# First mixer and first products of a two-layer decoder: VectorE's and ScalarE's queues laid by hand, and small modulation sums moved to ScalarE

## The chip, the cores and the metric

The kernel runs on one core of one Trainium2 chip. A core has TensorE (PE, matmuls), VectorE (DVE), ScalarE (ACT), GpSimd (POOL) and SyncE (SP, which here issues the loads and stores). Each engine takes its own queue in order; engines wait for each other by semaphores. The metric is the time of one execution in device microseconds (us), as the median of several runs.

## The reference

A decoder of two layers on 512 tokens of width 1024, in float32. Each layer has a mixer and an MLP, both behind an RMS norm whose result is scaled and shifted by a modulation that is computed from a vector `c`. The first layer's mixer is pooling: for each of four groups of 256 features a running mean over a window of 2, 4, 8 or 16 tokens, less the token itself, then a 256x256 product. The second layer's mixer is a gated unit (`sgu`), which the change does not touch.

```python
c_act = jax.nn.silu(c)
for i in range(DEPTH):
    mod = c_act @ ada_w[i] + ada_b[i]
    sh1, sc1, g1, sh2, sc2, g2 = jnp.split(mod, 6, axis=-1)
    h = modulate(rmsnorm(x, norm_mix_g[i]), sh1, sc1)
    ...
    x = x + g1[:, None, :] * y
    h = modulate(rmsnorm(x, norm_mlp_g[i]), sh2, sc2)
    x = x + g2[:, None, :] * sq_relu_mlp(h, mlp_w1[i], mlp_w2[i])
return rmsnorm(x, final_g)
```

`modulate(h, sh, sc)` is `h * (1 + sc) + sh`; `sq_relu_mlp` is `square(relu(h @ w1)) @ w2`.

## The kernel before

**Stages.** The kernel works through the first mixer (lines 177 to 376), the first products of the first MLP (the "sweep", lines 379 to 401), the rest of the first MLP, the second mixer and the second MLP. A large product is made of three matmuls in a fast format (`mm3`, lines 125 to 127): each operand is split into a high part (`h`, a copy by ScalarE in the fast type) and a low part (`l`, the remainder, by VectorE). `split` (lines 116 and 117) does it for weights.

**The modulation.** A column of 128 values of `mod` is the sum, over the 1024 entries of `c_act` (spread over all partitions as `cb`), of the products with a transposed weight tile. `column` (line 249) and `ada_tile` (line 147) load a 512 KB tile and do this in one VectorE instruction with an accumulator. `finish_mods` (lines 132 and 136) adds the bias and makes `scl = (1 + sc) * gain`.

**The first mixer.** `row`, `x` and the bands (triangles of 1/window, built by GpSimd) come first; `squares` (lines 209, 211) and `power` (line 168, on GpSimd) give each token's norm `rt`, which is multiplied into the bands (`bandr`, line 235). Then, for each group g of 256 features:

- `gains(g)`: the gate g1 of the group, spread over partitions and multiplied into the pooling weights `pw` (lines 298, 301). For g = 0 and 1 TensorE makes it (lines 285, 286); for g = 2 and 3 VectorE makes two columns, ScalarE writes them on a diagonal `dgg` (line 295) and TensorE spreads them (line 296).
- `windows(g)`: the windowed means by TensorE, straight from `x` (line 271).
- `modulation(g)`: four columns, bias and scale (lines 249, 257, 259).
- `pooled(g)`: the shift's part `b0` (lines 314, 315) and then ScalarE's scaling out of PSUM into `pd` (line 318).
- `group(g)`: the product (line 328), its addition to `x` (line 329) and the squares for the next norm (lines 209, 211). All squares write a common scratch tile `sq`, so they follow each other.
- `feature_major(g)`: TensorE's transposes of `x` (line 337) and ScalarE's copy into `xf` (line 338).

At the end `s3` collects the sums of squares (lines 364 to 366), `power` makes `r4`, four diagonals (lines 373, 375) and four small matmuls (line 376) spread it as `rb`.

**The sweep.** Step k (0 to 7) takes 128 features: two columns of modulation (`ada_tile`), the load and split of the weights `w1s[k]` (`sweep_w`, lines 387 to 391), `norm_fm` (line 381 `ht`, line 382 `hh`, line 383 `hl`) and 21 matmuls of 512 columns into seven PSUM banks.

**What sets the order.** TensorE's queue is in the order of the program (`manual_schedule(engines={PE})`). The queues of VectorE, ScalarE and SyncE are made by a scheduler, which may put an instruction of a later step ahead of one that is not ready by its own estimate. Weight and modulation tiles live in rotating buffers: `w4` (three of 4 KB per partition) and `wh`, `wl` (five each). `get_any` hands out these 13 in turn, in the order in which the program asks. A load waits in SyncE's queue until its buffer is free, and holds up the loads behind it.

```python
slots = [(w4, "w4")] * 3 + [(wts, "wh"), (wts, "wl")] * 5
...
for k in range(KD):
    for j in range(2):
        ada_tile(0, 24 + 2 * k + j, ada0[16 + 2 * k + j], get_any)
    wk = sweep_w(k)
    norm_fm(k)
    for f in range(SWEEP):
        mm3(sweep[f], cut(wk, ALL, slice(P * f, P * f + P)), (hh[:, k], hl[:, k]), k == 0, k == KD - 1)
```

Of the kernel before, what the change touches and what calls it, by code (L numbers as in the profile page):

```python
# [14 lines left out]
P = 128  # L15
# [28 lines left out]
def c_g(n, k):  # L44
    return 24 * n + 16 + k
# [3 lines left out]
def decoder_kernel(ctx: ExitStack, tc: tile.TileContext, xtok, vecs, rows, fgrow, ada0, adag, ada1, pool_w, w1s, w1, w2, w2e, w_v, w_u, w_o, wsT, lnp, bs, out):  # L49
# [127 lines left out]
    with tc.tile_pool(name="st", bufs=1) as st, tc.tile_pool(name="st2", bufs=2) as st2:  # L177
# [45 lines left out]
        for n in range(2):  # L223
            pc = bank("pc")
            T.matmul(pc, ones[0:1, :], row[0:1, D + S + S * n : D + 2 * S + S * n], start=True, stop=True)
            A.activation(psb[:, S * n : S * n + S], pc, AF.Copy)
# [4 lines left out]
        rt = power(v0, NT)  # L231

# [18 lines left out]
        def modulation(g):  # L251

            c = slice(4 * g, 4 * g + 4)
            pm = sm.tile([P, 4], F32, name="pm4", tag="pm4")
            for j in range(4):
                column(ada0[4 * g + j], pm[:, j : j + 1])
            V.tensor_tensor(mods[0][:, c], pm, vec[:, V_ADAB + c.start : V_ADAB + c.stop], ALU.add)
            k = slice(2 * g, 2 * g + 2)
# [3 lines left out]
        b0 = st.tile([P, KD], F32, name="b0")  # L262
        xf = st.tile([P, KD, S], F32, name="xf")
        ssg = st.tile([P, NT, 4], F32, name="ssg")

        def window(k):

            po = bank("pq")
            for t in range(NT):
                n = P if t == NT - 1 else W  # L270
                T.matmul(po[:, P * t : P * t + n], x[:, t, P * k : P * k + P], bandr[:, t, k // 2, 0:n], start=(t == 0), stop=(t == NT - 1), skip_group_check=True)  # L271
            return po


        ON_PE = 2

        def gains(g):

            po = bank("pg", xz)[:, 0:256]
            if g < ON_PE:  # L280
                for j in range(2):
                    r = get_any().rearrange("p (k c) -> p k c", k=4)
                    nc.sync.dma_start(r, adag[g, j])
                    for k in range(4):
                        T.matmul(po, cab[:, 4 * j + k], r[:, k], start=(j + k == 0), stop=False)
                T.matmul(po, ones[0:1, :], row[0:1, D + 256 * g : D + 256 * g + 256], start=False, stop=True)
            else:
                pm = sm.tile([P, 2], F32, name="pmg", tag="pmg")
                dg = st2.tile([P, 2, P], F32, name="dgg", tag="dgg")
                for j in range(2):  # L290
                    k = 2 * g + j
                    column(ada0[32 + k - 2 * ON_PE], pm[:, j : j + 1])
                V.tensor_tensor(pm, pm, vec[:, V_ADAB + c_g(0, 2 * g) : V_ADAB + c_g(0, 2 * g) + 2], ALU.add)
                for j in range(2):
                    A.activation(dg[:, j], ident, AF.Copy, scale=pm[:, j : j + 1])
                T.matmul(po, ones, dg, start=True, stop=True)
            gp = st2.tile([P, 256], F32, name="gp", tag="gp")
            V.tensor_tensor(gp, po, psb[:, 256 * g : 256 * g + 256], ALU.mult)
            c = slice(2 * g, 2 * g + 2)
            nc.sync.dma_start(pw[:, c], pool_w[:, c])  # L300
            V.tensor_tensor(pw[:, c], pw[:, c], gp.unsqueeze(1).to_broadcast([P, 2, 256]), ALU.mult)

        pqs, pds = {}, {}

        def windows(g):
            for k in (2 * g, 2 * g + 1):
                pqs[k] = window(k)

        def pooled(g):

            win = 2 << g

            bg, sh = b0[:, 2 * g : 2 * g + 2], mods[0][:, 4 * g + 1 : 4 * g + 4 : 2]
            V.tensor_scalar(bg, sh, float(win), 1.0 / win, ALU.mult, ALU.mult)
            V.tensor_tensor(bg, bg, sh, ALU.subtract)
# [4 lines left out]
        def group(g):  # L320

            c = slice(256 * g, 256 * g + 256)
            for h in range(2):
                po = bank("po", xz).rearrange("p (t c) -> p t c", t=2)
# [4 lines left out]
                V.tensor_tensor(x[:, 2 * h : 2 * h + 2, c], x[:, 2 * h : 2 * h + 2, c], po, ALU.add)  # L329
                for t in (2 * h, 2 * h + 1):  # L330
                    squares(ssg[:, t, g : g + 1], t, c, V if (g, t) in ((3, 1), (3, 3)) else A)

        def feature_major(g):
            for k in (2 * g, 2 * g + 1):
                px = bank("px")
                for t in range(NT):
                    T.transpose(px[:, P * t : P * t + P], x[:, t, P * k : P * k + P], ident)
                A.activation(xf[:, k], px, AF.Copy)
# [27 lines left out]
        V.tensor_tensor(s3, s3, ssg[:, :, 3], ALU.add)  # L366
        feature_major(3)
        r4 = power(s3, NT)
        diag = st.tile([P, NT, P], F32, name="diag")
        rb = bank("rb", xz)  # L370
        for t in range(NT):
# [4 lines left out]
            T.matmul(rb[:, tok[t]], ones, diag[:, t], start=True, stop=True)  # L376


        def norm_fm(k):
            t = st2.tile([P, S], F32, name="ht", tag="ht")  # L380
            V.scalar_tensor_tensor(t, xf[:, k], scl[0][1][:, k : k + 1], rb, ALU.mult, ALU.mult)
            A.activation(hh[:, k], t, AF.Identity, bias=mod(0, c_sh(1, k)))  # L382
            V.scalar_tensor_tensor(hl[:, k], t, mod(0, c_sh(1, k)), f32(hh[:, k]), ALU.add, ALU.subtract)  # L383

        def sweep_w(k):
            r = w4.tile([P, D], F32, name="raw", tag="w4")
            nc.sync.dma_start(r[:, 0 : P * SWEEP], w1s[k])
            h, l = wpair()
            c = slice(0, P * SWEEP)
            A.activation(h[:, c], r[:, c], AF.Copy)  # L390
            V.tensor_tensor(l[:, c], r[:, c], f32(h)[:, c], ALU.subtract)
            return h, l

        sweep = [bank("po") for _ in range(4)] + [bank("po", xz) for _ in range(SWEEP - 4)]
        for k in range(KD):
            for j in range(2):
                ada_tile(0, 24 + 2 * k + j, ada0[16 + 2 * k + j], get_any)
# [478 lines left out]
```

## Time and profile before

| | |
|---|---|
| time, three runs | 904.31 us median (904.25 to 906.77) |
| the profiled execution | 907.76 us, of which its span is 906.0 us |
| mean granted TensorE clock | 0.984 of full speed |
| TensorE (PE) busy | 870.8 us, 96% of the span |
| TensorE weight load (PEld) busy | 721.2 us, 80% |
| VectorE (DVE) busy | 654.2 us, 72% |
| ScalarE (ACT) busy | 414.0 us, 46% |
| GpSimd (POOL) busy | 53.3 us, 6% |
| read from HBM | 135.87 MB |

The span runs from the first to the last instruction of the profiled execution; the time includes what lies around it. Times are in us unless marked ns. L249 is line 249 of the kernel. A wait is put down to the instruction that came last. Busy time of an engine is an average over stages with different limits: what counts for the change is the stage ahead of the first products and the sweep itself, which end near 78.75 and 118 us.

### The profile page before, as it was taken

The page shows a single profiled execution, that of the slowest core. Times are in us where ns is not written, and L with a number is a line of the kernel's source. Part 1 is how long each engine was busy: PE and PEld are TensorE (multiplying, and loading weights), DVE is VectorE, ACT ScalarE, POOL GpSimd, SP SyncE. Part 2 cuts the span into 40 slices and gives each one's busy share as a digit, 9 for nine tenths or more (in the row PEclk, how much of TensorE's full clock was granted, in tenths as well). Part 3 has the DMA queues.
Part 4 walks back from the last instruction along what each step waited for, and adds up shares of the span by engine and source line. Part 5 has one row for each costly group of instructions (what it writes and reads, how often), then busy time and mean ns, then how long its engine had stood idle before and what let it go on. Part 6 is the DMA issues. An engine that isn't in the chain of part 4 may idle for free.

```text
span 906.0 us, 10439 instructions
## 1 busy us (share of the span) xinstructions
PE 870.8 (96%) x3980; PEld 721.2 (80%) x3980; DVE 654.2 (72%) x862; ACT 414.0 (46%) x585; POOL 53.3 (6%) x102
## 2 busy tenths in 40 slices
PE   7766999999999999999999999999999999999996
PEld 5655888788888888888878888988887888888885
DVE  4878787768888888947798745547667675767954
ACT  4253375544444445337333326634545444445421
POOL 6000001100000000000410001000004000000000
PEclk9896999999999999999999999999999999999998
DMA  8955773454365350724548204632343033112212
GB/s 339 407 190 207 248 267 109 145 203 163 119 213 196 123 187 23 243 83 149 186 146 281 97 24 176 225 134 71 140 174 105 33 144 150 47 57 84 94 47 93
DMA packets 35476, 138.65 MB, mean 153 GB/s; under 512 B 3937, under 2 KB 4065, under 8 KB 32225
## 3 DMA queue, kind: packets, MB, share of 16 engines
q1 hardware_dynamic: 35282, 137.72, 42.2%
q8 instruction: 31, 0.51, 0.2%
q10 hardware_dynamic: 144, 0.26, 0.1%
q14 instruction: 19, 0.16, 0.1%
HBM read 135.87 MB, written 2.10 MB: 152 GB/s over the span
## 4 chain that ended last, share of the span: by engine, by line
PE 89%; DVE 4%; DMA 3%; ACT 2%; issue 1%; SPq 0%; POOL 0%; POOLq 0%; DVEq 0%; ACTq 0%
PE po L126 17%; PE po L127 17%; PE po L125 17%; PE pm L126 11%; PE pm L127 11%; PE pm L125 11%; DMA ada<-in_ada 1%; DMA wh<-in_ada 1%; PE po L725 1%; PE pq L271 1%; DMA raw<-in_w1s 1%; PE pb L161 1%; DMA wl<-in_ada 0%; PE po L328 0%; PE px L634 0%
## 5 line engine op out<-in xcount | busy, mean ns | idle before, releaser
L125 PE MATMUL po<-hh,wl 128*128 128x512 f32 (+1 forms) x608 | 232.4, 382 | 2.7 <-ACT hh L382 2.7
L126 PE MATMUL po<-hl,wh 128*128 128x512 f32 (+1 forms) x608 | 230.8, 380 | 3.1 <-DVE hl L383 1.9
L127 PE MATMUL po<-hh,wh 128*128 128x512 f32 (+1 forms) x608 | 230.3, 379 | 0.0
L117 DVE TENSOR_TENSOR wl<-b,wh 128x1024 fp32r<-128x1024 f32 x84 | 102.6, 1223 | 71.4 <-ACT wh L116 71.4
L117 DVE TENSOR_TENSOR wl<-raw,wh 128x1024 fp32r<-128x1024 f32 x89 | 108.7, 1222 | 49.2 <-ACT wh L116 48.9
L126 PEld LDWEIGHTS po<-hl,wh 128*128 128x128 f32 x608 | 114.8, 189 | 25.8 <-DVE hl L383 2.4
L125 PEld LDWEIGHTS po<-hh,wl 128*128 128x128 f32 x608 | 114.8, 189 | 25.1 <-ACT hh L382 3.0
L127 PEld LDWEIGHTS po<-hh,wh 128*128 128x128 f32 x608 | 114.8, 189 | 21.3
L127 PE MATMUL pm<-wh,oh 128*128 128x512 f32 x336 | 130.7, 389 | 0.0
L125 PE MATMUL pm<-wh,ol 128*128 128x512 f32 x336 | 130.7, 389 | 0.0
L126 PE MATMUL pm<-wl,oh 128*128 128x512 f32 x336 | 130.7, 389 | 0.0
L116 ACT ACTIVATE wh<-raw 128x1024 fp32r<-128x1024 f32 x89 | 94.1, 1057 | 62.3 <-PE pm L127 33.7
L429 ACT ACTIVATE g<-po 128x512 f32<-128x512 f32 x64 | 38.0, 599 | 166.8 <-PE po L127 166.8
L116 ACT ACTIVATE wh<-b 128x1024 fp32r<-128x1024 f32 x84 | 88.4, 1053 | 14.1 <-PE pm L127 9.3
L147 DVE SCALAR_TENSOR_TENSOR ada<-ada,cb 128x1024 f32<-128x1024 f32 x60 | 73.1, 1220 | 17.0 <-DMA ada<-in_ada 16.9
L126 PEld LDWEIGHTS pm<-wl,oh 128*128 128x128 f32 x336 | 63.1, 188 | 13.1
L125 PEld LDWEIGHTS pm<-wh,ol 128*128 128x128 f32 x336 | 63.1, 188 | 13.1
L127 PEld LDWEIGHTS pm<-wh,oh 128*128 128x128 f32 x336 | 63.1, 188 | 13.1
L611 ACT ACTIVATE tmp<-x 128x512 f32<-128x512 f32 (+1 forms) x25 | 15.3, 612 | 64.6 <-DVE x L607 64.6
L529 DVE TENSOR_TENSOR y<-y,pm 128x512 f32<-128x512 f32 x68 | 43.4, 680 | 0.0
L430 ACT ACTIVATE g<-g 128x512 f32<-128x512 f32 x64 | 39.6, 625 | 0.0
L158 POOL TENSOR_SCALAR dg<-ident,mods 128x128 f32<-128x128 f32 x24 | 25.6, 1083 | 215.3 <-DVE wl L117 215.3
(168 smaller groups left out, 1151.2 us busy)
## 6 DMA issues: line engine op xcount, KB each, us to landing
ada<-in_ada SPq DMA_DIRECT2D x64, 512.0 KB, 3.7
raw<-in_w SPq DMA_DIRECT2D x57, 512.0 KB, 3.3
b<-in_w SPq DMA_DIRECT2D x24, 1024.0 KB, 4.9
raw<-in_w2e SPq DMA_DIRECT2D x16, 512.0 KB, 3.3
wh<-in_ada SPq DMA_DIRECT2D x14, 512.0 KB, 9.6
wl<-in_ada SPq DMA_DIRECT2D x14, 512.0 KB, 9.6
ur<-in_w_u SPq DMA_DIRECT2D x8, 512.0 KB, 4.8
raw<-in_w_v SPq DMA_DIRECT2D x8, 512.0 KB, 4.8
```

What stands on the lines that cost most here:

```text
L116: A.activation(h, r, AF.Copy)
L117: V.tensor_tensor(l, r, f32(h), ALU.subtract)
L125: T.matmul(o, wl, mh, start=first, stop=False, **kw)
L126: T.matmul(o, wh, ml, start=False, stop=False, **kw)
L127: T.matmul(o, wh, mh, start=False, stop=last, **kw)
L147: V.scalar_tensor_tensor(r, r, 1.0, cb, ALU.mult, ALU.mult, accum_out=pmv[i, b][:, j : j + 1])
L158: G.tensor_scalar(dg[:, k], ident, cols[:, k : k + 1], None, ALU.mult)
L161: T.matmul(po, ones, dg[:, 4 * n : 4 * n + 4], start=True, stop=True)
L429: A.activation(t, po, AF.Relu)
L430: A.activation(t, t, AF.Square)
L529: V.tensor_tensor(yt, yt, banks[hf], ALU.add)
L611: A.activation(tmp, xt, AF.Square, scale=D**-0.5, accum_out=s[:, len(cs) : len(cs) + 1])
```

## The change

The first mixer and the sweep are put into a second `manual_schedule`, for VectorE and ScalarE, so their queues follow the program. The functions are cut into smaller ones (`modulation` into `m` and `fin`, `gains` into `gains`, `gain_cols`, `gain_spread` and `weigh`, `group` into `product`, `add` and `sums_of`, `feature_major` into `turn` and `turned`) and called in a list written by hand. In TensorE's queue `windows(1)` goes ahead of `gains(1)`, the spread of the gains of g = 2 and 3 behind the product of the group before, and the transposes move a little. SyncE's queue is still the scheduler's, which follows the new times that it estimates. In the sweep, `ada` replaces `ada_tile`: bias and scale are three small ScalarE instructions where they were two on VectorE; columns, load and split of step k + 1 are asked for within step k. The sum of squares, `power` and everything behind the sweep are as they were.

```diff
-    with tc.tile_pool(name="st", bufs=1) as st, tc.tile_pool(name="st2", bufs=2) as st2:
+    with (
+        tc.tile_pool(name="st", bufs=1) as st,
+        tc.tile_pool(name="st2", bufs=2) as st2,
+        tc.manual_schedule(engines={mybir.EngineType.DVE, mybir.EngineType.Activation}),
+    ):
...
-        for n in range(2):
-            pc = bank("pc")
-            T.matmul(pc, ones[0:1, :], row[0:1, S * n : S * n + S], start=True, stop=True)
-            A.activation(cb[:, S * n : S * n + S], pc, AF.Silu)
         psb = st.tile([P, D], F32, name="psb")
...
+        def spread_row(o, c0, f):
+            for n in range(2):
+                pc = bank("pc")
+                T.matmul(pc, ones[0:1, :], row[0:1, c0 + S * n : c0 + S * n + S], start=True, stop=True)
+                A.activation(o[:, S * n : S * n + S], pc, f)
+        spread_row(cb, 0, AF.Silu)
...
+        spread_row(psb, D + S, AF.Copy)
...
+        def m(g, *js):
+            if g not in pm4:
+                pm4[g] = sm.tile([P, 4], F32, name="pm4", tag="pm4")
+            for j in js:
+                column(ada0[4 * g + j], pm4[g][:, j : j + 1])
+        def fin(g):
+            win = 2 << g
+            c, k = slice(4 * g, 4 * g + 4), slice(2 * g, 2 * g + 2)
+            V.tensor_tensor(mods[0][:, c], pm4[g], vec[:, V_ADAB + c.start : V_ADAB + c.stop], ALU.add)
             V.scalar_tensor_tensor(scl[0][0][:, k], mods[0][:, c.start : c.stop : 2], 1.0, vec[:, V_MIX + k.start : V_MIX + k.stop], ALU.add, ALU.mult)
+            bg, sh = b0[:, k], mods[0][:, c.start + 1 : c.stop : 2]
+            V.tensor_scalar(bg, sh, float(win), 1.0 / win, ALU.mult, ALU.mult)
+            V.tensor_tensor(bg, bg, sh, ALU.subtract)
...
+        def gain_cols(g):
+            pm = sm.tile([P, 2], F32, name="pmg", tag="pmg")
+            dg = dgs[g] = st2.tile([P, 2, P], F32, name="dgg", tag="dgg")
+            for j in range(2):
+                column(ada0[32 + 2 * (g - 2) + j], pm[:, j : j + 1])
+            load_pw(g)
+            V.tensor_tensor(pm, pm, vec[:, V_ADAB + c_g(0, 2 * g) : V_ADAB + c_g(0, 2 * g) + 2], ALU.add)
+            for j in range(2):
+                A.activation(dg[:, j], ident, AF.Copy, scale=pm[:, j : j + 1])
+        def gain_spread(g):
+            pgs[g] = bank("pg", xz)[:, 0:256]
+            T.matmul(pgs[g], ones, dgs.pop(g), start=True, stop=True)
+        def weigh(g):
+            gp = st2.tile([P, 256], F32, name="gp", tag="gp")
+            V.tensor_tensor(gp, pgs.pop(g), psb[:, 256 * g : 256 * g + 256], ALU.mult)
...
+        def ada(k, j):
+            if j == 0:
+                pm2[k] = sm.tile([P, 2], F32, name="pm2", tag="pmv")
+            column(ada0[16 + 2 * k + j], pm2[k][:, j : j + 1])
+            if j == 1:
+                for q in range(2):
+                    c, b = c_sc(1, k) + q, V_ADAB + c_sc(1, k) + q
+                    A.activation(mod(0, c), pm2[k][:, q : q + 1], AF.Identity, bias=vec[:, b : b + 1])
+                g = vec[:, V_MLP + k : V_MLP + k + 1]
+                A.activation(scl[0][1][:, k : k + 1], mod(0, c_sc(1, k)), AF.Identity, scale=g, bias=g)
+        def sweep_load(k):
+            r = w4.tile([P, D], F32, name="raw", tag="w4")
+            nc.sync.dma_start(r[:, 0 : P * SWEEP], w1s[k])
+            wk[k] = r[:, 0 : P * SWEEP], *(t[:, 0 : P * SWEEP] for t in wpair())
+        def sweep_hi(k):
+            A.activation(wk[k][1], wk[k][0], AF.Copy)
+        def sweep_lo(k):
+            V.tensor_tensor(wk[k][2], wk[k][0], f32(wk[k][1]), ALU.subtract)
...
         gains(0)
         windows(0)
-        modulation(0)
+        m(0, 0, 1)
+        weigh(0)
+        m(0, 2, 3)
+        fin(0)
         pooled(0)
+        windows(1)
         gains(1)
-        windows(1)
-        group(0)
-        modulation(1)
+        m(1, 0, 1)
+        product(0)
+        weigh(1)
+        m(1, 2)
+        add(0, 0)
+        add(0, 1)
+        m(1, 3)
+        fin(1)
         pooled(1)
-        gains(2)
+        for t in range(NT):
+            sums_of(0, t)
         windows(2)
-        group(1)
-        feature_major(0)
-        modulation(2)
+        gain_cols(2)
+        product(1)
+        turn(0)
+        turned(0)
+        gain_spread(2)
+        m(2, 0)
+        add(1, 0)
+        weigh(2)
+        m(2, 1)
+        add(1, 1)
+        m(2, 2, 3)
+        fin(2)
         pooled(2)
-        gains(3)
+        for t in range(NT):
+            sums_of(1, t)
         windows(3)
-        group(2)
-        feature_major(1)
-        modulation(3)
+        turn(1)
+        turned(1)
+        gain_cols(3)
+        product(2)
+        gain_spread(3)
+        m(3, 0)
+        weigh(3)
+        m(3, 1)
+        add(2, 0)
+        add(2, 1)
+        m(3, 2, 3)
+        fin(3)
         pooled(3)
-        feature_major(2)
-        group(3)
+        for t in range(NT):
+            sums_of(2, t)
+        turn(2)
+        turned(2)
         s3 = sm.tile([P, NT], F32, name="s3", tag="rv4")
         V.tensor_reduce(s3, ssg[:, :, 0:3], mybir.AxisListType.X, ALU.add)
         V.tensor_scalar(s3, s3, RMS_EPS, None, ALU.add)
+        ada(0, 0)
+        ada(0, 1)
+        sweep_load(0)
+        product(3)
+        add(3, 0)
+        sums_of(3, 0)
+        sums_of(3, 1, V)
+        sweep_hi(0)
+        add(3, 1)
+        sums_of(3, 2)
+        sums_of(3, 3, V)
         V.tensor_tensor(s3, s3, ssg[:, :, 3], ALU.add)
-        feature_major(3)
         r4 = power(s3, NT)
+        sweep_lo(0)
+        turn(3)
...
+        turned(3)
+        ada(1, 0)
+        sweep = [bank("po") for _ in range(4)] + [bank("po", xz) for _ in range(SWEEP - 4)]
+        for k in range(KD):
             t = st2.tile([P, S], F32, name="ht", tag="ht")
             V.scalar_tensor_tensor(t, xf[:, k], scl[0][1][:, k : k + 1], rb, ALU.mult, ALU.mult)
             A.activation(hh[:, k], t, AF.Identity, bias=mod(0, c_sh(1, k)))
+            if k and k + 1 < KD:
+                ada(k + 1, 0)
             V.scalar_tensor_tensor(hl[:, k], t, mod(0, c_sh(1, k)), f32(hh[:, k]), ALU.add, ALU.subtract)
-        def sweep_w(k):
-            r = w4.tile([P, D], F32, name="raw", tag="w4")
-            nc.sync.dma_start(r[:, 0 : P * SWEEP], w1s[k])
-            h, l = wpair()
-            c = slice(0, P * SWEEP)
-            A.activation(h[:, c], r[:, c], AF.Copy)
-            V.tensor_tensor(l[:, c], r[:, c], f32(h)[:, c], ALU.subtract)
-            return h, l
-        sweep = [bank("po") for _ in range(4)] + [bank("po", xz) for _ in range(SWEEP - 4)]
-        for k in range(KD):
-            for j in range(2):
-                ada_tile(0, 24 + 2 * k + j, ada0[16 + 2 * k + j], get_any)
-            wk = sweep_w(k)
-            norm_fm(k)
+            if k + 1 < KD:
+                sweep_load(k + 1)
+                sweep_hi(k + 1)
+                ada(k + 1, 1)
+                sweep_lo(k + 1)
             for f in range(SWEEP):
-                mm3(sweep[f], cut(wk, ALL, slice(P * f, P * f + P)), (hh[:, k], hl[:, k]), k == 0, k == KD - 1)
+                mm3(sweep[f], cut(wk[k][1:], ALL, slice(P * f, P * f + P)), (hh[:, k], hl[:, k]), k == 0, k == KD - 1)
     def mlp(i, first, extra, last, ending):
```

More of the change, by code (lines that the diff above doesn't have):

```diff
@@ L249, in column @@
             V.scalar_tensor_tensor(r, r, 1.0, cb, ALU.mult, ALU.mult, accum_out=out)
[L251 to L258, printed above, removed]
+        pm4, b0 = {}, st.tile([P, KD], F32, name="b0")
@@ L261, in decoder_kernel @@
         pw = st.tile([P, KD, 256], F32, name="pw")
[L262 to L272, printed above, removed]
@@ L275, in decoder_kernel @@
[L275 to L280, printed above, removed]
-                for j in range(2):
[L282 to L298, printed above, removed]
@@ L299, in gains, with load_pw @@
+        pgs, dgs = {}, {}
+        def load_pw(g):
             c = slice(2 * g, 2 * g + 2)
             nc.sync.dma_start(pw[:, c], pool_w[:, c])
+        def gains(g):
+            po = pgs[g] = bank("pg", xz)[:, 0:256]
+            for j in range(2):
+                r = get_any().rearrange("p (k c) -> p k c", k=4)
+                nc.sync.dma_start(r, adag[g, j])
+                for k in range(4):
+                    T.matmul(po, cab[:, 4 * j + k], r[:, k], start=(j + k == 0), stop=False)
+            T.matmul(po, ones[0:1, :], row[0:1, D + 256 * g : D + 256 * g + 256], start=False, stop=True)
+            load_pw(g)
@@ L328, in group @@
                         T.matmul(po[:, q], pds[2 * g + j][:, P * t : P * t + P], pw[:, 2 * g + j], start=(j == 0), stop=(j == 1))
[L329 to L333, printed above, removed]
+        xf = st.tile([P, KD, S], F32, name="xf")
+        ssg = st.tile([P, NT, 4], F32, name="ssg")
@@ L334, in feature_major, with add, sums_of, turn @@
+        def add(g, h):
+            c = slice(256 * g, 256 * g + 256)
+            V.tensor_tensor(x[:, 2 * h : 2 * h + 2, c], x[:, 2 * h : 2 * h + 2, c], pos.pop((g, h)), ALU.add)
+        def sums_of(g, t, on=A):
+            squares(ssg[:, t, g : g + 1], t, slice(256 * g, 256 * g + 256), on)
+        pxs = {}
+        def turn(g):
             for k in (2 * g, 2 * g + 1):
-                px = bank("px")
+                pxs[k] = bank("px")
                 for t in range(NT):
-                    T.transpose(px[:, P * t : P * t + P], x[:, t, P * k : P * k + P], ident)
@@ L360, in decoder_kernel @@
+        weigh(3)
[4 more added lines that the diff above has]
+        fin(3)
         pooled(3)
[L361 to L362 removed]
+        for t in range(NT):
+            sums_of(2, t)
+        turn(2)
+        turned(2)
         s3 = sm.tile([P, NT], F32, name="s3", tag="rv4")
```

31 lines of the change are left out of this document (15 added, 16 removed).

## The prediction

> **What bounds the kernel now.** I read the table of who waited for whom on TensorE first, because TensorE is busy in 96% of the span and only its idle time can be won or lost.
>
> ```profile
> PE pg L296 <- ACT dgg L295: 8.4, 2, 5.0
> PE rb L376 <- ACT diag L375: 6.4, 1, 6.4
> PE po L125 <- ACT hh L382: 2.7, 1, 2.7
> PE po L126 <- DVE hl L383: 1.9, 1, 1.9
> PE po L126 <- DVE hl L643: 1.2, 2, 0.9
> ```
>
> Columns: us in total, times, longest. The waits on `dgg`, `diag`, `hh` and `hl` L383 all lie ahead of the second matmul of the sweep, at 78.75 us. After that TensorE waits 1.4 us in all (the last line and 0.2 elsewhere). So the change can win only ahead of 78.75, and anything that makes the sweep stall is lost in full. Next, busy time by stretches (us, then busy and instructions of each engine, granted TensorE clock, DMA share, GB/s):
>
> ```profile
> 14.70:78.70 64.00, 41.38 (x198) 33.98 (x196) 52.66 (x116) 25.69 (x60) 1.02 (x1) 0.84 0.80 307
> 78.70:118.40 39.70, 39.65 (x169) 32.72 (x170) 29.08 (x47) 16.01 (x22) 0.00 (x0) 0.96 0.67 238
> ```
>
> Before the sweep VectorE (third) is the fullest, 52.66 of 64.0 us; in the sweep TensorE is (39.65 of 39.70), and VectorE has slack. The chain of waits tells what closes the stage (start, us, what):
>
> ```profile
> 48.08 1.22 PE pg L296 x2
> ...
> 60.14 5.88 DMA raw<-in_w1s
> 66.04 0.96 ACT wh L390
> ...
> 69.76 1.03 POOL rr L168
> ...
> 72.46 4.32 DMA wl<-in_ada
> 76.80 1.23 DVE wl L147 x2
> 78.03 0.68 DVE hl L383
> ```
>
> VectorE and ScalarE do work of later sweep steps (L390 split, L147 modulation columns) ahead of the sums, `r4` and the first `hl`: two loads sit in a chain that needs neither.
>
> Last, the timeline of loads (SPq) and VectorE in the sweep, for the price of a late load:
>
> ```profile
> 97.85 0.33 SPq L143 DMA_DIRECT2D wl<-in_ada  x1
> ...
> 102.19 1.22 DVE L147 SCALAR_TENSOR_TENSOR wl<-wl,cb 128x1024 f32<-128x1024 f32 x1 [1.30 <-DMA wl<-in_ada]
> ...
> 84.57 0.33 SPq L143 DMA_DIRECT2D wl<-in_ada  x1
> ...
> 87.96 1.23 DVE L147 SCALAR_TENSOR_TENSOR wl<-wl,cb 128x1024 f32<-128x1024 f32 x1 [1.27 <-DMA wl<-in_ada]
> ```
>
> From issue to use: 4.34 us behind another load, 3.39 alone.
>
> **Part 1, the head (to 78.75).** Work: in the old order VectorE does eight columns of k = 0 to 3 (L147, 1.15 from one to the next), four splits L391 (1.01) and two `ht` (0.67) before `hl` of k = 0. The new order keeps three columns, one split and one `ht`. Moved behind: 5 x 1.15 + 3 x 1.01 + 0.67 = 9.4. The modulation sums of step 0 (L132, L136) go to ScalarE, 0.2 less. So VectorE has 52.7 - 9.6 = 43.1 us to do from 14.7 on.
>
> Waits: the old stage had 11.3 (64.0 - 52.7). The new ones, walked along the fixed queues:
> - The first loads are unchanged: 1.7 at 21.4 (1.6 before, `wl` L249 on its load), and 0.1 at 16.
> - `weigh(2)` stands in VectorE's queue ahead of `add(1, 1)` and the columns of g = 2, and needs the spread of the gains, which TensorE does after `product(1)` and eight transposes. VectorE arrives at 35.7 (b0 of g = 1 at 31.3, three columns 3.45, small ones 0.3, an add 0.6). TensorE: `pd` of g = 1 written by 32.8, product 3.62 (L328 at 26.16), transposes 1.04, spread 0.63: 38.0. Wait 2.3 (before 1.0).
> - `weigh(3)`: VectorE arrives at 47.6. ScalarE has `pd` of g = 2 ready at 45.3, then four squares (0.54 each), two `xf` (0.49), two `dgg` (0.29): 49.1, spread 0.6: 49.7. Wait 2.1 (before 1.2).
> - `s3` is now queued ahead of the columns of k = 0 and `add(3, 0)`, and waits for ScalarE's two `pd` (1.35) and four squares (2.2) of g = 2: 3.6. Nothing did before: the old order filled this with columns.
> - the two squares on VectorE wait for ScalarE's (shared scratch `sq`): 0.65 + 0.6; POOL's power 1.0; `rb` 1.0; `hh` 0.8.
>
> Sum 13.8, and 14.7 + 43.1 + 13.8 = 71.6 for `hl` of k = 0, if TensorE runs at full clock in both `weigh` waits. In the old trace it did not: the 16 passes of L271 took 2.18 us at 24.14 but 3.94 at 35.78, after 4.98 idle. At half clock the first wait grows by some 2.3 (half of 4.7), the second by 3.4 (3.62 doubled, less the cover of squares), and `product(3)` holds `add(3, 1)` by 0.8: 78.1. The new order leaves TensorE idle too (some 1 us before `product(1)`, near 3 before `product(2)`), so neither end is excluded; I take the middle, 75.0. Gain 3.75, between 0.6 and 7.1.
>
> **Part 2, the sweep.** TensorE needs 4.76 us a step (21 matmuls of 0.227). VectorE's queue per step is now fixed: `ht`, column (k+1, 0), `hl`, column (k+1, 1), split of k+1, that is 0.67 + 1.15 + 0.67 + 1.15 + 1.01 = 4.65. That fits only if nothing waits. But the column loads wait. In the queue of loads as built, the load of column (3, 1) stands behind the sweep weights of k = 5, and those wait for a buffer of `w4` that the split of k = 2 frees on VectorE. The same holds for (4, 1) behind k = 6 and the split of 3, (5, 1) behind k = 7 and the split of 4; (6, 1) stands behind the load of column (7, 1), in `w4` too, and so behind the split of 5. Column (k+1, 1) is itself ahead of the split of k+1: a closed loop. One turn: 0.05 (semaphore) + 0.43 (two issues) + 4.34 (landing behind another load) + 1.15 (column) + 1.01 (split) = 6.98. Behind the waiting column stand the split, `ht` and `hl` of that step, and TensorE waits for those. In the old trace the same loads ran two or three steps ahead: TensorE never waited in the sweep.
>
> Stall: steps 3 to 6 come every 6.98 instead of 4.76: 4 x 2.22 = 8.9. Step 2: after `hl` of k = 0, column, split, `ht`, column (3.9) free the buffer for k = 4, then 0.05 + 0.43 + 4.34 + 1.15 + 1.01, and `ht`, column, `hl` (2.5): 13.4, against two steps of TensorE with the half-clock start seen at 78.75 (9.5 + 1.4): 2.5. In all 11.4. Steps 1 and 7 are TensorE's own.
>
> A sentence of the Trainium skill beside it, page "DMA: Bandwidth & Descriptors", whose fit is 2.0 us + bytes / 436e3: two loads of 448 and 512 KB one after the other would land 3.8 us after the second issue, the turn would be 6.5 and the stall near 9. The rows (4.34) decide here.
>
> The small sums on ScalarE: three of 128x1 a step. The trace has no such row; the nearest are 0.21 (128x8, `ca`) and 0.60 (128x512). So 0.6 to 1.8 a step beside `hh` 0.72 and the split 0.95, in 6.98: hidden, cost 0 (uncovered, at most 1.8 on one step, the last). VectorE loses two of 0.15.
>
> After the sweep TensorE's queue is the same and it hardly waited, so nothing is given back.
>
> **Sum.** -3.75 + 11.4 = +7.7. The profiled execution took 907.76 (span 906.0), which becomes 915.4; it lies 3.4 above the median 904.31, to which the same +7.7 gives **912.0**.
>
> **Rivals.**
> - Faster: the loads do not close a loop, the sweep hides all. Then only the head counts, 904.3 - 3.75 = 900.6 (897 at full clock). It decides from a turn under 4.76 on, that is a landing within 2.1 us. For it: VectorE's 4.65. Against: no row of this size is under 3.2. 5%.
> - It cancels: full clock in the head (-7.1) and loads landing as if alone (3.39: turn 6.03, stall 4 x 1.27 + 1.5 = 6.6): 903.8. 8%.
> - Stop and go drops the clock in the sweep: TensorE is idle 2.2 of every 7 us. A half-clock step lasts up to 9.5 instead of 4.76; since 6.98 is waited out anyway, the excess is 2.5 on each step it falls on: on two, +5, 917. Against: at 16.9 to 20.3, with 1.9 busy of 3.4 us, passes stayed fast. 12%. The Trainium skill, "TensorE: Matmul & The Clock Gate", section "A second HAM failure mode: psum-queue depth-cycling", says short idle gaps between groups can make the clock swing; the trace does not yet show such a case.
> - The head wins nothing (78.1 or later, half clock throughout): 904.3 - 0.6 + 11.4 = 915.1. 10%.
>
> **How the numbers follow.** My forecast, both parts as walked, 65%: 908.5 to 916. The slower rivals make 87% slower in all. About 0.3% (2.7 us) can be told from no change: faster by more 5%, within 8%, slower 87%. Lower end 906.5 (head 71.6 with a turn of 6.5: -7.1 + 9); upper 918 (head 78.1, landing 4.8, clock +1.5). The corners left out are 903.8 and, with every load as late as 5.88 (60.14), 922.
>
> **What would show it.** `hl` of k = 0 at 72 to 78, no L147 or split of later steps before `r4`; VectorE waiting about 2 to 5 us for `pg` twice and 3.6 for ScalarE at `s3`; TensorE waiting some 2 us in each of sweep steps 2 to 6, the column waiting for its load each time, the sweep 51 us long instead of 39.4; no new wait later. I am wrong if TensorE runs the sweep without waits, if the loads of (3, 1) to (6, 1) are issued before the splits, or if `hl` comes after 78.75.

## The result, and the profile after

| | before | after |
|---|---|---|
| median | 905.54 us (904.25 to 908.16, 4 runs) | 918.81 us (918.33 to 919.36, 4 runs) |
| ratio to before | | 1.0143, 95% interval 1.0116 to 1.017 |
| profiled execution (span) | 907.76 (906.0) | 919.2 (917.1) |
| TensorE: second matmul of the sweep, end of the sweep | 78.75, 118.15 | 75.78, 129.31 |
| from the end of the sweep to the end of the span | 787.85 | 787.8 |

The changed kernel is slower, by more than the 0.3% that can be told. The head got 3.0 us shorter, the sweep 14.1 us longer (53.5 instead of 39.4), and nothing changed behind it. TensorE's table of waits up to 140 us (us in total, times, longest), kernel after:

```profile
PE po L125 <- ACT hh L479: 7.7, 5, 2.3
PE px L357 <- ACT pd L330: 4.8, 1, 4.8
PE px L357 <- DVE x L345: 4.5, 3, 3.1
PE po L338 <- ACT pd L330: 4.4, 2, 2.9
...
PE rb L470 <- ACT diag L469: 2.6, 1, 2.6
PE po L126 <- DVE hl L482: 2.5, 5, 0.6
```

TensorE's waits for `hh` are five now: one at the sweep's start, as before, and four inside it. Those for `hl` are five too, all inside the sweep; before there was one, at its start. Together TensorE waits 8.6 us behind its second matmul, where it waited for nothing before. In the rest of the 14.1 us it is busy longer (45.00 us instead of 39.65): two stretches are at half clock, and a matmul that starts after a wait takes 0.50 us by itself instead of 0.23 in a row. That the lower clock has no price of its own is worked out further down. The busy time by stretches, head and sweep, kernel after (us; busy and instructions of PE, PEld, DVE, ACT, POOL; granted TensorE clock, DMA share, GB/s):

```profile
14.70:75.75 61.05, 43.00 (x201) 34.71 (x199) 42.95 (x93) 24.44 (x61) 1.80 (x1) 0.85 0.62 246
75.75:129.30 53.55, 45.00 (x168) 34.03 (x168) 34.03 (x49) 21.41 (x45) 0.00 (x0) 0.92 0.60 208
```

In the head VectorE has 42.95 us to do, down from 52.66. In the sweep it is busy for 34.03 of 53.55 us, TensorE for 45.00, the loads for 60%: no engine is full, which is what a loop of waits looks like. The chain of waits of the kernel after shows the loop (start, us, what; "issue" stands where VectorE is already in the column that it had waited for):

```profile
75.64 1.23 DVE ada L255 x2
76.87 1.00 DVE wl L389
77.87 0.66 DVE ht L478
78.53 1.16 DVE ada L255 x2
79.70 0.33 SPq L382
80.08 6.47 DMA wh<-in_ada
86.61 1.11 issue
87.81 1.01 DVE wl L389
88.84 0.33 SPq L382
89.27 4.18 DMA wh<-in_ada
93.64 1.06 issue
94.78 1.00 DVE wl L389
95.78 0.66 DVE ht L478
...
103.21 4.65 DMA wh<-in_ada
```

Read a turn from 87.81: the split (L389) ends at 88.82 and frees a `w4` buffer; at 88.84 SyncE issues the sweep weights that waited for it (L382), at 89.27 the column's load behind them; it lands after 4.18 us; the column (93.55 to 94.78) and the next split follow, 6.97 us after the last one. VectorE waits for hardly anything but these loads, in the table of its waits from 76 to 125 us of the same kernel:

```profile
DVE wh L255 <- DMA wh<-in_ada: 15.8, 5, 6.2
DVE ht L478 <- ACT scl L378: 0.2, 1, 0.2
```

### The profile page after: what moved, and what is told of

Same layout as the page of the kernel before. It is cut to its first block, busy times and chain, and to the rows that moved or that the text cites. A ratio compares the mean times of both kernels' runs of the same rounds, so it can differ in the third digit from the quotient of the medians.

```text
span 917.1 us, 10446 instructions
## 1 busy us (share of the span) xinstructions
PE 877.8 (96%) x3980; PEld 723.3 (79%) x3980; DVE 653.8 (71%) x846; ACT 419.9 (46%) x609; POOL 54.3 (6%) x102
## 4 chain that ended last, share of the span: by engine, by line
PE 87%; DVE 5%; DMA 3%; ACT 2%; issue 1%; SPq 0%; POOL 0%; POOLq 0%; DVEq 0%; ACTq 0%
PE po L126 16%; PE po L127 16%; PE po L125 16%; PE pm L126 11%; PE pm L127 11%; PE pm L125 11%; DMA wh<-in_ada 2%; PE po L338 1%; PE pg L291 1%; DMA ada<-in_adag 1%; PE po L813 1%; DVE wl L255 1%; PE pb L161 1%; DVE wh L255 1%; DVE wl L389 1%
## 5 line engine op out<-in xcount | busy, mean ns | idle before, releaser
L147 DVE SCALAR_TENSOR_TENSOR ada<-ada,cb 128x1024 f32<-128x1024 f32 x56 | 68.2, 1221 | 16.6 <-DMA ada<-in_ada 16.5
```

The lines of the kernel that those rows point to most:

```text
L147: V.scalar_tensor_tensor(r, r, 1.0, cb, ALU.mult, ALU.mult, accum_out=pmv[i, b][:, j : j + 1])
```

## The experiments

Times are compared with runs of the kernel before on the same chip; these had medians of 907.26 in 25 runs (for loads in program order, the split ahead, the sums on VectorE again, and the head alone), 908.17 in 25 runs (for the sums in the kernel before, the sweep alone, `s3` later and both `weigh` later) and 908.09 in 7 runs (for the sweep alone with the loads in order, and TensorE kept busy).

### The loop through the loads

**Loads in program order.** VectorE's and ScalarE's queues are not touched; SyncE's too is taken from the scheduler.

```diff
-        tc.manual_schedule(engines={mybir.EngineType.DVE, mybir.EngineType.Activation}),
+        tc.manual_schedule(engines={mybir.EngineType.DVE, mybir.EngineType.Activation, mybir.EngineType.SP}),
```

> VectorE's and ScalarE's queues stay as the change laid them; only SyncE's queue follows the program too, so that the load of column (k+1, 1) no longer stands behind the sweep weights of k + 3. Theory (the closed loop through the loads): the waits of steps 2 to 6 go, the sweep shrinks from 53.5 us to 40.5 to 42 (39.4 as before, 1.4 for a start at half clock), and the time from 918.8 to 904 to 907. Rival 1 (the laid order of VectorE, 4.65 us a step, is itself what stalls): the sweep stays above 50 us, 916 to 920. Rival 2 (the granted clock drops in the sweep by itself): some half-clock steps stay, 908 to 914.

Measured: 905.56 us (904.6 to 908.22, 10 runs), ratio to before 0.9986 (0.9966 to 1.0006). The sweep, by stretches of this kernel:

```profile
76.40:117.20 40.80, 40.80 (x169) 33.31 (x169) 34.92 (x50) 21.56 (x45) 0.00 (x0) 0.93 0.80 278
```

TensorE waits for nothing in the sweep; VectorE's order is the same and its work nearly so (34.9 us here, 34.0 in the kernel after). The timeline of loads of this kernel shows why (start, us, queue, operation, how many):

```profile
77.52 0.33 SPq L382 DMA_DIRECT2D raw<-in_w1s  x1
77.90 0.43 SPq L254 DMA_DIRECT2D wh<-in_ada  x1
78.38 0.42 SPq L254 DMA_DIRECT2D wl<-in_ada  x1
78.90 0.38 SPq L382 DMA_DIRECT2D raw<-in_w1s  x1
```

One sweep weight, then the two columns that are needed next, then the next weight. In the kernel after the same view has

```profile
76.90 3.13 SPq L382 DMA_DIRECT2D raw<-in_w1s  x3
80.08 0.43 SPq L254 DMA_DIRECT2D wh<-in_ada  x1
```

three weights, the last of them for a buffer that came free only at 79.70, ahead of the column. So the queue of loads, not VectorE's order, made the loss: rival 1 falls. Rival 2 falls too: TensorE is at half clock only in the first step.

**The split ahead of the column.** The work stays the same, but a buffer comes free without the column.

```diff
-                ada(k + 1, 1)
                 sweep_lo(k + 1)
+                ada(k + 1, 1)
```

> The change, but VectorE does the split of k + 1 ahead of column (k+1, 1), so that the buffer for the sweep weights of k + 4 comes free without waiting for that column. The work on VectorE is the same, 4.65 us a step. Theory (loop): a turn now takes two steps, 0.05 + 0.43 + 4.34 + 1.15 + 0.67 + 1.15 + 0.67 + 1.01 = 9.5 us, 4.75 a step, about TensorE's own 4.76; sweep 42 to 45 us, time 907 to 911. Rival (VectorE's amount of work or the laid order as such): no change, 917 to 920.

Measured: 910.7 us (908.49 to 912.62, 10 runs), 1.0028 (1.001 to 1.0047); sweep 44.8 us (75.62 to 120.42). The loop loosened as the theory says. (In the profiled execution, 912.62 us, 790.4 us lie behind the sweep, 2.6 more than in the kernel after; TensorE is at half clock there from 566 to 569 us.) What is left is another wait, in the table of VectorE's waits from 76 to 120 us of this kernel:

```profile
DVE ht L478 <- ACT scl L378: 3.8, 6, 0.6
DVE wh L255 <- DMA wh<-in_ada: 2.1, 1, 2.1
```

With the column directly ahead of `ht`, the three small ScalarE sums lie between them: 0.6 us a step. In the kernel after they cost 0.2 in all, since the split covers them.

**The small sums on VectorE again**, with `finish_mods` in place of the three ScalarE instructions.

```diff
             if j == 1:
-                for q in range(2):
-                    c, b = c_sc(1, k) + q, V_ADAB + c_sc(1, k) + q
-                    A.activation(mod(0, c), pm2[k][:, q : q + 1], AF.Identity, bias=vec[:, b : b + 1])
-                g = vec[:, V_MLP + k : V_MLP + k + 1]
-                A.activation(scl[0][1][:, k : k + 1], mod(0, c_sc(1, k)), AF.Identity, scale=g, bias=g)
+                finish_mods(0, 12 + k, pm2[k])
```

> The change, but the small modulation sums of the sweep are made on VectorE again (two instructions of some 0.15 us a step where ScalarE has three). Theory (loop): they lie between column (k+1, 1) and the split of k + 1, so each of four turns of the loop gets 0.15 to 0.3 longer: 918.8 plus 0.6 to 1.2, so 919.4 to 920. Rival (the three sums on ScalarE hold up hh and the split, at 0.2 to 0.6 each): the sweep gets 3 to 9 us shorter, 910 to 916.

Measured: 919.18 us (918.8 to 919.66, 4 runs). The four turns (ends of `hl` from 89.70 to 119.54) took 7.46 us each, 0.36 more than the 7.1 of the kernel after (91.28 to 119.70); step 2 was shorter by 1.1 us (`hl` of k = 2 14.4 after that of k = 0, against 15.6), since the column's load was issued at 78.24 here, ahead of the third sweep weight at 79.66. So the sweep grew by only 0.4 and the time ends just below the theory's band. The rival falls: ScalarE's sums did not cause the loss.

**The same small sums on ScalarE, in the kernel before.** The diff is that of the last experiment the other way round, within `ada_tile`.

> The kernel before, with the small modulation sums of the sweep alone moved to ScalarE (three instructions a step for two on VectorE). Theory: hidden on both engines, so no change beyond what a new order by the scheduler brings, 0.3% either way, 903 to 907. Rival (they delay hh and the splits on ScalarE): 2 to 5 us slower, 907.5 to 910.

Measured: 904.73 us (901.81 to 906.93, 10 runs), 0.9971 (0.9953 to 0.9988). The rival falls. The second sweep matmul came at 77.25 instead of 78.75: the scheduler makes another order for the whole head, so the 0.3% can't be put down to the sums themselves.

### The head

**Laid by hand up to the sweep only.**

```diff
-        tc.manual_schedule(engines={mybir.EngineType.DVE, mybir.EngineType.Activation}),
...
+        laid = tc.manual_schedule(engines={mybir.EngineType.DVE, mybir.EngineType.Activation})
+        laid.__enter__()
...
         ada(1, 0)
+        laid.__exit__(None, None, None)
```

> The queues are laid by hand only up to the sweep; in the sweep the scheduler orders VectorE and ScalarE again, and it loads by its own times. Theory: the head's gain of 3.0 us is real and separate, the sweep is 39.4 to 42 us, so 902.5 to 905.5 against 905.5 of the kernel before. Rival (the head's gain is borrowed: the 9.4 us of VectorE's work moved behind the first hl comes back as waits in the sweep whatever orders it): 906 to 912.

Measured: 907.34 us (905.53 to 909.27, 10 runs), 1.0005 (0.9985 to 1.0025): no gain, which is the rival's number. The second sweep matmul came at 75.83, but the sweep took 41.9 us. Its first step (75.83 to 82.83) was 0.9 longer than the 6.1 of before, from a longer stretch at half clock, and a step with a wait of 1.2 us for `hl` was 1.6 longer than the others. So of the 2.9 us won 2.5 were given back in the sweep. Another 0.7 lie behind it (788.6 us from its end, 787.85 before); why stays open. The loss in the sweep fits the rival's account (work that the old order had done early has to be done there), but only the step with the wait speaks for it; the rest is the clock.

**Laid by hand in the sweep only.** The program of the change, with the scheduler ordering VectorE and ScalarE in the head.

```diff
-        tc.manual_schedule(engines={mybir.EngineType.DVE, mybir.EngineType.Activation}),
...
+        laid = tc.manual_schedule(engines={mybir.EngineType.DVE, mybir.EngineType.Activation})
+        laid.__enter__()
         sweep = [bank("po") for _ in range(4)] + [bank("po", xz) for _ in range(SWEEP - 4)]
...
+        laid.__exit__(None, None, None)
```

> The change's program, but the queues are laid by hand only in the sweep; the scheduler orders VectorE and ScalarE in the head. Theory (loop): the loads of the sweep stand as in the change, so each turn takes 7 us again, sweep 50 to 54 us; with hl of k = 0 anywhere from 71 to 79 that is 913 to 921. Rival (the loss comes from the laid head, whose order pushes columns and splits into the sweep): the scheduler has pulled such work ahead again, sweep 40 to 43 us, 902 to 908.

Measured: 912.38 us (910.02 to 913.62, 10 runs), 1.005 (1.0034 to 1.0066), just below the theory's band since the head came out earlier than forecast. By stretches, this kernel:

```profile
14.70:68.70 54.00, 40.52 (x200) 32.70 (x199) 41.54 (x93) 24.63 (x61) 1.02 (x1) 0.89 0.71 278
68.70:121.80 53.10, 44.94 (x169) 33.89 (x169) 34.01 (x49) 21.48 (x45) 0.00 (x0) 0.92 0.61 211
```

The sweep is that of the kernel after, loop and all. The head is 7.1 us shorter than the laid one: VectorE waits 12.5 us in it, in the laid head 18.1, and has 1.4 us less to do (41.54 against 42.95). It is also 10.0 us shorter than that of the kernel before (second sweep matmul at 68.72 instead of 78.75), with 11.1 us less of VectorE's work ahead of the sweep. So it is not the order written by hand in the head that makes the head short: what goes with the short head is that later steps' columns and splits stay out of it, and the order written by hand gave most of that back. The change also moves instructions in TensorE's queue; their share was not tried alone. Where the laid head loses is in VectorE's own table of waits, 14.70 to 75.75, kernel after:

```profile
DVE gp L312 <- PE pg L307: 7.0, 2, 5.0
DVE s L446 <- ACT sq L214: 3.5, 1, 3.5
```

The two `weigh` and `s3`: 10.5 us at three places where the order written by hand lets a waiting instruction stand ahead of work that is ready. With the scheduler's head neither line is in the table; its longest waits there are 4.6 us for `po` and 2.8 for the gains of g = 0 and 1.

**The same, with the loads in program order.**

```diff
+        tc.manual_schedule(engines={mybir.EngineType.SP}),
...
-        laid = tc.manual_schedule(engines={mybir.EngineType.DVE, mybir.EngineType.Activation})
+        laid = tc.manual_schedule(engines={mybir.EngineType.DVE, mybir.EngineType.Activation, mybir.EngineType.SP})
```

> As the run with only the sweep laid by hand (912.4; hl of k = 0 started at 67.9, sweep 53.0 us), but SyncE's queue follows the program. Theory (two separate effects: the loop through the loads costs the sweep some 12 us, and the laid head is some 7 us later than the scheduler's order of the same program): sweep 40 to 41.5 us, hl of k = 0 at 67.5 to 69, time 898 to 901. Rival (the early hl of that run comes from loads or columns that the scheduler's order of SyncE had brought forward): hl of k = 0 at 71 to 76, 902 to 907.

Measured: 899.01 us (898.06 to 900.6, 4 runs), 0.9907 (0.9886 to 0.9929). Second sweep matmul at 68.79, sweep 40.4 us. The two effects are separate: the loop costs 12.6 us of sweep here (53.0 against 40.4) and 12.7 with the laid head (53.5 against 40.8).

**`s3` later** (on the kernel with the loads in order).

```diff
-        V.tensor_reduce(s3, ssg[:, :, 0:3], mybir.AxisListType.X, ALU.add)
-        V.tensor_scalar(s3, s3, RMS_EPS, None, ALU.add)
         ada(0, 0)
...
         add(3, 0)
+        V.tensor_reduce(s3, ssg[:, :, 0:3], mybir.AxisListType.X, ALU.add)
+        V.tensor_scalar(s3, s3, RMS_EPS, None, ALU.add)
```

> On the kernel with the loads in program order (905.6): the two s3 instructions are asked for behind add(3, 0) instead of ahead of the columns of k = 0, so VectorE no longer waits 3.6 us for ScalarE's squares there. Theory (VectorE's queue sets the end of the head, and a microsecond there is one at the end): the two columns (2.3 us) lie in the old wait, hl of k = 0 comes 2 to 3 us earlier, time 902.5 to 904. Rival (the clock: TensorE's clock came back at 81 to 82 us in every run so far, whether its second sweep matmul was at 75.8 or at 78.8, so half of an earlier start is spent at half clock): 904 to 905.5.

Measured: 903.9 us (902.45 to 905.29, 10 runs), 0.9957 (0.9942 to 0.9972); second sweep matmul at 73.09, 3.3 us earlier, first step 6.5. In the trace all of it arrives at the end of the sweep (3.4 earlier), and 0.6 is lost behind it. The medians differ by 1.7, and by 2.6 if each is taken against its own runs of before (0.0029 of 907): at the border of the two bands, which the times do not tell apart. The rival's premise falls, though: the clock came back at 76.9 here, not at 81 to 82.

**Both `weigh` later too.**

```diff
         m(2, 0)
         add(1, 0)
-        weigh(2)
-        m(2, 1)
+        m(2, 1, 2)
         add(1, 1)
-        m(2, 2, 3)
+        weigh(2)
+        m(2, 3)
...
-        m(3, 0)
-        weigh(3)
-        m(3, 1)
+        m(3, 0, 1)
+        m(3, 2, 3)
         add(2, 0)
+        weigh(3)
         add(2, 1)
-        m(3, 2, 3)
```

> As the run with s3 late, and weigh of g = 2 and 3 asked for behind more columns of their own group (weigh(2) behind add(1, 1), weigh(3) behind all four columns and add(2, 0)), so that the waits of 2.1 and 5.0 us for the spread gains are filled with work. Theory (VectorE's queue sets the head's end): of 10.7 us of waits some 8 to 10 go, hl of k = 0 at 66 to 69, time 895.5 to 899. Rival (TensorE, idle and at half clock in these stretches, and ScalarE's pd then set the end): 900 to 904.

Measured: 895.44 us (894.6 to 896.73, 4 runs), 0.9865 (0.9839 to 0.9891). By stretches, and TensorE's waits up to 140 us, this kernel:

```profile
14.70:65.45 50.75, 39.77 (x200) 32.23 (x199) 42.56 (x93) 24.15 (x61) 1.80 (x1) 0.90 0.75 295
65.45:105.40 39.95, 39.95 (x169) 32.88 (x169) 34.72 (x50) 21.45 (x45) 0.00 (x0) 0.95 0.82 289
```

```profile
PE px L357 <- ACT pd L330: 2.7, 1, 2.7
PE rb L469 <- ACT diag L468: 2.6, 1, 2.6
PE po L338 <- ACT pd L330: 2.0, 2, 1.5
PE px L357 <- DVE x L345: 2.0, 3, 1.2
```

VectorE's 42.6 us of work stand in 50.75 us, and TensorE waits less with it: 4.8 became 2.7, 4.4 became 2.0, 4.5 became 2.0. This version is faster than both kernels.

### The clock and the spread of the kernel before

**TensorE kept busy ahead of the sweep** (on the kernel with both `weigh` late).

```diff
         rb = bank("rb", xz)
+        for _ in range(5):
+            T.matmul(rb[:, 0:256], ident, cab[:, 0:2], start=True, stop=True)
...
         sweep = [bank("po") for _ in range(4)] + [bank("po", xz) for _ in range(SWEEP - 4)]
+        for _ in range(3):
+            T.matmul(sweep[0][:, 0:256], ident, cab[:, 0:2], start=True, stop=True)
```

> The kernel with both weighs late (895.4), and eight matmuls of 256 columns whose results nobody reads, in TensorE's two idle stretches ahead of the sweep (2.65 us before rb, 1.65 us before hh): five into the bank of rb, three into the first bank of the sweep; both are overwritten. Theory (the half-clock start of the sweep comes from these idle stretches and costs 1.2 to 2.5 us): the first step takes 4.8 us instead of 6.5 to 7.3, time 892.5 to 894.5. Rival (the clock had been set back earlier and the eight matmuls at half clock come too late for rb): 895.5 to 897.

Measured: 894.95 us (894.32 to 895.46, 4 runs), not told apart from 895.44; the spans are both 893.5. TensorE's timeline, this kernel (start, us, what, idle time before):

```profile
60.02 2.32 PE L465 MATMUL rb<-cab,ident 128*128 128x256 f32 x10
62.83 1.16 PE L471 MATMUL rb<-diag,ones 128*128 128x128 f32 x8 [0.48 <-ACT diag L470]
63.82 1.46 PE L478 MATMUL po<-cab,ident 128*128 128x256 f32 x6
65.64 0.50 PE L125 MATMUL po<-hh,wl 128*128 128x512 f32 x1 [0.36 <-ACT hh L482]
66.43 0.50 PE L126 MATMUL po<-hl,wh 128*128 128x512 f32 x1 [0.28 <-DVE hl L485]
```

The clock stayed full, and the first step took 4.7 us instead of 6.5: that half of the theory holds. The time did not follow; it lies between the two bands. In this execution the transposes ahead of `rb`, and so ahead of the first added matmul, already ended 1.1 us later (60.2 against 59.1), and TensorE then waited 0.9 us for `hl`, 0.6 of it in steps 2 and 3 (5.5 and 5.3 us long): VectorE, with 4.65 us of work a step and 1.5 us of waits for two columns' loads, had not caught up. What a full clock would bring with VectorE out of the way stays open.

**Two more traces of the kernel before.** The edit is none.

> The kernel before, unchanged, for another trace of it: its executions so far lie between 904.1 and 910.5, the profiled one at 907.76. Theory (the spread is made ahead of the sweep, where TensorE is idle and its clock drops by stretches): a trace with another time has the end of the sweep earlier or later than 118.15 by that difference, and from there to the end the same 788 us within 0.5. Rival (the spread lies in the long part behind the sweep): the sweep ends at 118.2 within 0.5, and the rest differs.

> As the run beside it, for a third trace of the kernel before: by the theory the end of the sweep moves with the time, one for one; by the rival the end of the sweep stays at 118.2.

Measured: 909.47 us (span 907.8), the sweep ends at 119.72; and 908.75 us (907.0), 119.29. The first trace had 907.76 (906.0) and 118.15. What follows the sweep takes 788.1, 787.7 and 787.85 us: the spread between these traces lies ahead of the end of the sweep, as the theory says. The granted clock (third column from the right) by stretches, first trace, then the last one:

```profile
81.00:82.00 1.00, 1.00 (x4) 0.81 (x3) 1.00 (x4) 0.73 (x1) 0.00 (x0) 0.63 0.00 0
82.00:83.00 1.00, 1.00 (x7) 0.79 (x6) 1.00 (x3) 0.63 (x2) 0.00 (x0) 1.00 0.00 0
```

```profile
82.00:83.00 1.00, 1.00 (x4) 0.73 (x3) 1.00 (x4) 0.63 (x2) 0.00 (x0) 0.50 0.00 0
83.00:84.00 1.00, 1.00 (x4) 0.81 (x3) 1.00 (x2) 0.49 (x1) 0.00 (x0) 0.50 0.00 0
84.00:85.00 1.00, 1.00 (x5) 0.83 (x5) 0.96 (x3) 0.00 (x0) 0.00 (x0) 0.98 0.00 0
```

The sweep's second matmul starts at 78.75 and 78.93, nearly the same; the clock comes back at 81.7 in one and at 84.0 in the other, and the first step takes 6.1 or 7.0 us. No trace of an execution near 904.3 was taken.

## Why the prediction was right and wrong

The forecast was 912.0, the measurement 918.81: the direction and the mechanism were right, the size was not. It lies 0.8 above the range's upper end. Two terms of the sum carry the miss: the load in step 2 of the sweep, and the base that the sum was added to. Point by point:

- **The head's walk held, its clock was luck.** The single waits: `weigh(2)` 2.00 (2.3 at full clock), `weigh(3)` 4.96 (2.1 at full, 5.5 at half clock; TensorE was at half clock from 43.8 to 50.7), `s3` 3.53 (3.6), POOL 0.9, `rb` 0.9, `hh` 0.8. VectorE had 42.95 us to do (43.1). The prediction could not tell the clock and took 75.0 as the middle between full and half clock in both `weigh` waits. What came was full clock in the first and half clock in the second, which by its own terms (13.8 + 3.4 us of waits) is 75.0 too: that the middle fitted is luck.
- **The head's gain was booked 0.8 too high.** The work of 43.1 is that of the stretch up to 78.7, which ends with `hl` of k = 0, so the 75.0 of the sum is the end of that `hl`. It started at 74.97 and ended at 75.72, with 18.1 us of VectorE's waits ahead of it instead of 17.2. From matmul to matmul the gain is 78.75 - 75.78 = 3.0, not 3.75.
- **The closed loop exists, and its turn was right.** Forecast 6.98; the waiting columns start 6.97, 6.96, 7.45 and 7.04 us apart. It is shown to be the cause: with SyncE's queue alone in program order the sweep went from 53.5 to 40.8. An estimate from the Trainium skill ("DMA: Bandwidth & Descriptors", section "Anatomy of one DMA — SWDGE (gpsimd) path", its fit of 2.0 us + bytes / 436e3 for a load issued from GpSimd) gave a turn of 6.5; the measured landings of 4.18 to 4.65 behind another load decide against it here.
- **The step that failed is step 2 of the sweep.** The prediction priced the load of column (2, 1) at 4.34, as behind one other load; it stood behind three sweep weights, issued at 76.90, 77.90 and 79.70, and landed after 6.47, so `hl` of k = 2 came 15.6 us after that of k = 0 instead of 13.4. That is 2.2 of the 2.7 us by which the sweep's loss (14.1 instead of 11.4) was mis-sized; the four turns make 0.5 (28.4 against 27.9), mostly the one of 7.45, and steps 6 and 7 make 0.1.
- **The half clock in the sweep had no price.** It lasted from 71.1 to 81.4 and made the first step 2.5 us longer than a step at full clock (1.3 in the kernel before, taken as 1.4), but `hl` of k = 2 is set by loads and VectorE, and waits that out. The same goes for a half-clock stretch at 91.6 to 95.0, inside a step that the loop held at 7.3 us: TensorE, slower there, then waited only 0.3 us in step 3, against 2.9, 1.6, 2.1 and 1.7 in steps 2, 4, 5 and 6 (forecast: some 2 in each). So the rival "stop and go drops the clock in the sweep" happened once, without a price.
- **The base was off by 3.0.** The forecast took the profiled execution of before as 3.4 above its median (907.76 against 904.31, of three runs) and took those 3.4 off the changed kernel too. The changed kernel's profiled execution lies 0.4 above its median. The kernel before spreads over 904.1 to 910.5, with medians of 907.26 and 908.17 of 25 runs each, so three runs were a poor median. Between the two profiled executions the loss is 11.4 us, where 7.7 were forecast. Why the changed kernel spreads over 1 us only stays open: the loop absorbs a late TensorE in the kernel after, but the run with the sweep laid alone has the loop and spreads over 3.6.
- 0.8 + 2.7 + 3.0 = 6.5 of the 6.8 us; the remaining 0.3 is time outside the span (2.1 against 1.8).
- **The small ScalarE sums: cost 0, right here.** The kernel after shows 0.2 us of waits for them; where the split no longer covers them they cost 3.8.
- **After the sweep nothing was given back**, as forecast.
- Of the rivals, the two in which the loop vanished or shrank fell, and so did the one in which the head wins nothing. What the first of them gave as the head's worth fell as well: without the loop, the head's gain arrives in part or not at all (905.56 and 907.34 for 907.26): 900.6 was too hopeful, since part of the earlier start falls into a stretch at half clock (first steps of 7.3 and 7.0 us instead of 6.1).
- **Slips that change no reading.** The terms given for the ends of the range add up to 906.2 and to 918.4 (918.9 with the later landing in step 2 as well), not to 906.5 and 918. Loads of 512 KB land in 3.0 us later in the trace of before, so 3.2 is not their least. TensorE is busy for 2.2 us from 16.9 to 20.3, not 1.9.

## What to carry to other kernels

A hand-laid order is only as good as the queues that are not laid: take loads into the same order, and look in each load queue for a transfer that waits for a buffer ahead of one that the buffer's owner needs. When costing such a loop, count for every turn how many loads are in front, the first turn above all. In an order written by hand, every instruction that waits for another engine is a place where ready work behind it stands still; moving three of them behind ready columns took the time from 905.56 to 895.44 us here. And try the scheduler's order on the same program before crediting the one written by hand: its head was 7.1 us shorter.

## What the runs showed of the hardware

- **Landing time grows with the loads in front.** For tiles of 448 or 512 KB in the sweep of the kernel after, from issue to landing: 3.1 to 3.5 us alone, 4.1 to 4.7 behind one other, 4.8 to 5.7 behind two, 6.5 and 7.2 behind three (the first of the three ended 0.3 us after the issue of the one that took 6.5); about 1 us for each load in front. With the loads in program order the first burst lies there too (4.34, 5.54 and 6.15 behind one, two and three); at 98 to 99 us two loads took 6.5 and 7.2, each with three others still on the way.
- **When the clock comes back does not follow one for one from when the work starts.** In the kernel before it came back at 81.7, 84.0 and 84.6 in three traces whose sweep started within 0.5 us; in the kernel after at 81.4, though its sweep started 3.0 earlier. From 20 us to the sweep's end the half-clock stretches last 6.8, 6.8, 10.2 and 3.4 us in the kernel after and 6.8, 3.4 and 13.7 in the kernel before: multiples of 3.4 us. The Trainium skill ("TensorE: Matmul & The Clock Gate", section "What's actually happening") says that activity is judged in free-running windows of about 3.4 us; the jumps of 2.3 and 2.9 us between executions of one program agree with windows that are not tied to the program's start. With the loads in program order the sweep's second matmul came at 76.41, 2.3 to 2.8 us earlier than in the three traces of before, and the sweep ended 1.0, 2.1 and 2.6 us earlier.
